# Second half of the output in one bank for each token block, the last in quarters; final sums of two blocks on ScalarE and GpSimd; eight gate stores from GpSimd's queue

## The chip, the core and the metric

The kernel runs on one core of a Trainium2 chip. A core has TensorE (matrix products, PE in the profile, with its weight loads as PEld), VectorE (DVE), ScalarE (ACT), GpSimd (POOL) and SyncE (SP), which here only issues DMAs. TensorE writes its products to PSUM, eight banks of 128 partitions by 512 float32; the other tiles lie in SBUF. Each engine works through its own instructions in order; semaphores join them. The metric is the time of one execution on the device in microseconds.

## What is computed

One layer of a hybrid encoder over 2048 tokens of width 1024, with 16 learned tokens ahead. The reference, cut:

```python
u = rms_norm(h, pre_g)
proj = u @ w_in
glu_a, glu_b, conv_gate, q, k, v, sb_gate = jnp.split(proj, ..., axis=-1)
c = glu_a * jax.nn.sigmoid(glu_b)
c = causal_depthwise_conv(c, conv_w, conv_b)                 # width 31
c = jax.nn.silu(layer_norm(c, conv_ln_g, conv_ln_b))
c = (c @ w_pw2 + b_pw2) * jax.nn.silu(conv_gate)
s = stick_breaking_attention(heads(q), heads(k), heads(v))   # 8 heads of 64
s = s.reshape(...) * jax.nn.silu(sb_gate)
mixed = jnp.concatenate([c, s], axis=-1) @ w_out
return h + rms_norm(mixed, post_g)
```

The change touches the last two lines for the last 512 tokens, and the storing of `silu(sb_gate)`.

## The kernel before

The tokens are worked in four chunks of 512 (`TC`). For each chunk there are input projections, convolution, attention over all keys so far, and the output projection. A float32 product is made of three passes: both factors are split in a high and a low part (ScalarE rounds, VectorE or GpSimd subtracts; "hi", "lo"), and high x high, high x low and low x high are added in one PSUM bank. In the profile every instruction has line 218, that of a recording helper; operations are told apart by their tiles.

The order of the instructions comes from a planner that runs when the program is built. It keeps an estimated time for each engine and merges two streams of TensorE work, the attention and a filler (projections, convolution, output projection); small jobs on other engines are put in with `when` once their inputs are expected. The order is thus fixed in the program.

*PSUM.* The eight banks are four tags (`BANKS`): "mm" 2, "T" 4, "av" 1, "cv" 1. "av" holds a head's attention sum, "cv" the running convolution while there is one.

*Gates.* `sb_gate(c)` (line 1073) projects the four gates of chunk c; each is stored to `gscr` in DRAM (line 1079) by SP's queue, which also loads weights ("wr", "w"), keys and values. They are read back much later.

*The end of the last chunk.* The mixed input has eight blocks of 128 channels; the last one (k = 7, heads 6 and 7) comes last, so everything else is done ahead of it. `out_part` (line 1600) sums the first seven blocks: for output columns 0 to 511 into SBUF ("tok"), for columns 512 to 1023 in `late` (line 1621) into PSUM banks that stay open. There a bank holds 256 columns (`OC`) of two token blocks of 128 tokens: `late(0)` fills "cv" and "mm" for blocks 0 and 1, `late(1)` "mm" and "T" for blocks 2 and 3. The second is run in part before and in part inside `out_last`.

`out_last` (line 1631) runs when the last mixed block is there, in the order written at lines 1691 to 1714: `first(tb)` multiplies the last block for columns 0 to 511, `second(i)` adds it to the open banks of blocks 2i and 2i + 1. `add_first` adds the bank to "tok", ScalarE squares it with a sum over the row ("sq"), VectorE multiplies by the gain ("uh", `post_g`); `add_second` squares and multiplies two pieces of 256 from the banks. `rate` adds the four partial sums (VectorE) and takes the power -0.5 (GpSimd, "st"). `give_out` makes the final sum `y * rate + x` on VectorE, two halves of 512 columns in "ul", and stores each by SP.

Two instructions on different engines that read one bank are kept apart by semaphores: VectorE's multiplication waits for ScalarE's square of the same bank.

Of the kernel before, what the change touches and what calls it, by code (L numbers as in the profile page):

```python
# [14 lines left out]
AF = mybir.ActivationFunctionType  # L15
ALU = mybir.AluOpType
# [3 lines left out]
P = 128  # L20
D = 1024
KD = D // P
SEQ = 2048
NM = 16
TC = 512
NCH = SEQ // TC
NTB = TC // P
# [7 lines left out]
OC = 256  # L35
# [231 lines left out]
def trunk(ctx: ExitStack, tc: tile.TileContext, x, xturn, xlater, meta, cpack, post_g, wpack, out):  # L267
# [16 lines left out]
    def when(what, ins, outs=(), engine=None, date=0.0, tag=None):  # L284
        soon.append(Later(clock, what, ins, outs, engine, date, tag))

    pe = Engine(clock, nc.tensor, pe_cost, 0.15, run)
    dve = Engine(clock, nc.vector, dve_cost, 0.04, run)
    act = Engine(clock, nc.scalar, act_cost, 0.04, run)
    pool = Engine(clock, nc.gpsimd, pool_cost, 0.04, run)  # L290
    sp = Engine(clock, nc.sync, sp_cost, 0.0, run)
# [24 lines left out]
    def T(tag, shape, bufs, dt=F32):  # L316
        room(tag, bufs)
        t = sb.tile(shape, dt, tag=tag, name=tag, bufs=bufs)
        clock.take(tag, bufs, t.name)
        return t  # L320

    def PT(tag, shape):
        bufs = BANKS[tag]
        room(tag, bufs)
        t = ps.tile(shape, F32, tag=tag, name=tag, bufs=bufs)
        clock.take(tag, bufs, t.name)
        return t
# [3 lines left out]
    def need(*aps, tag=None, given=None, evs=0, n=1):  # L331

        def at():
            if given and not given():
                return 1e6
            t = max([clock.at(a) for a in aps] + [0.0])
            if tag:
                t = max(t, clock.next_free(tag, n))  # L340
            if evs:

                t = max(t, clock.next_free("ev", evs) - 1.0)
            return t + slack[0]

        return at
# [6 lines left out]
    o = NJ * CW  # L353
# [116 lines left out]
    def finish_off(pieces):  # L470

        while True:
            try:
                next(pieces)
            except StopIteration as e:
                return e.value
# [116 lines left out]
    def release():  # L593
        held.pop()
        tags.popleft()
        prepare()
# [476 lines left out]
    def sb_gate(c):  # L1073
        for j in range(NJ):
            def ev_g(pt, o, n):
                sg = ev()[:, :TC]
                act.activation(sg, pt, AF.Sigmoid)
                dve.tensor_tensor(sg, pt, sg, op=ALU.mult)
                when(lambda j=j: sp.dma_start(gscr[c, j], sg), [sg], ["g"])

            yield from proj(c, G_SG + j, ev_g, False)

# [2 lines left out]
    keep = {("z", -1): True}  # L1085
# [487 lines left out]
    def out_products(w, mix, ks, half, whole=True, bank=None, there=None, tag="mm", free=None):  # L1573


        fresh = bank is None
        for i, k in enumerate(ks):
            wh, wl = (t[:, k % 2, :] for t in w[k // 2])
            if k % 2 == 0:
                pair = ks[i : i + 2]  # L1580
                if there:
                    yield need(given=lambda: all(there(kk) for kk in pair))
                nxt = [m for kk in pair for m in mix(kk)]
                yield need(wh, wl, *nxt, tag=None if bank is not None else tag)
            if bank is None:
                bank = PT(tag, [P, 2, OC])
            for b in range(2):
                tb = 2 * half + b
                mh, ml = (t[:, tb * P : (tb + 1) * P] for t in mix(k))
                o = bank[:, b, :]  # L1590


                pe.matmul(o, mh, wh, start=(fresh and i == 0 and b == 0), stop=False)
                pe.matmul(o, mh, wl, start=False, stop=False)
                pe.matmul(o, ml, wh, start=False, stop=(whole and i == len(ks) - 1 and b == 1))
            if (half if free is None else free) and (k % 2 or i == len(ks) - 1):
                release()
        return bank

    def out_part(y, c):  # L1600

        yield need(given=lambda: ("conv", c) in keep)
        mix = lambda k: mixc[c][k] if k < NJ else mixs[c][k - NJ]
        there = lambda k: k < NJ or k - NJ in mixs[c]
        for n in range(0, D // 2, OC):
            w = weights(w_out, n, OC, 0, KD - 1)
            ks, banks = range(KD - 1), [None, None]
            if n == 0:  # L1610

                for i in range(2):
                    banks[i] = yield from out_products(
                        w, mix, range(KD - 2), i, False, there=there
                    )
                ks = range(KD - 2, KD - 1)
            for i in range(2):
                b = yield from out_products(w, mix, ks, i, True, banks[i], there)
                act.activation(y[i][:, :, n : n + OC], b, AF.Copy)

        def late(i, tags):
            for e in range(2):
                w = weights(w_out, D // 2 + e * OC, OC, 0, KD - 1)
                keep["o", i, e] = yield from out_products(
                    w, mix, range(KD - 1), i, False, tag=tags[e], free=True
                )

        yield from late(0, ("cv", "mm"))
        keep["rest"] = late(1, ("mm", "T"))

    def out_last(y, mh, ml):


        def products(o, tb, wh, wl, start, stop):
            h, l = (t[:, tb * P : (tb + 1) * P] for t in (mh, ml))
            pe.matmul(o, h, wh, start=start, stop=False)
            pe.matmul(o, h, wl, start=False, stop=False)
            pe.matmul(o, l, wh, start=False, stop=stop)

        pg = keep["pg"]  # L1640
        w0, w1 = keep["w", 0], keep["w", 1]
        sums, rates = T("sq2", [P, NTB, 4], 1), {}
        pool.memset(sums[:, :, 3:], 1e-6)

        def first(tb):
            a = PT("T", [P, TC])
            products(a, tb, *w0, True, True)
            return a

        def second(i):  # L1650
            for e in range(2):
                for b in range(2):
                    w = (t[:, e * OC : (e + 1) * OC] for t in w1)
                    products(keep["o", i, e][:, b], 2 * i + b, *w, False, b == 1)

        def square(tb, src, n):
            junk = T("ev", [P, TC], EV, BF16)[:, : src.shape[1]]

            act.activation(
                junk, src, AF.Square, scale=D ** -0.5, accum_out=sums[:, tb, n : n + 1]  # L1660
            )

        def add_first(tb, a):

            yt = y[tb // 2][:, tb % 2, 0:TC]
            dve.tensor_tensor(yt, yt, a, op=ALU.add)
            square(tb, yt, 0)
            dve.tensor_tensor(yt, yt, pg[:, 0], op=ALU.mult)

        def add_second(tb):  # L1670
            yt = y[tb // 2][:, tb % 2, TC:]
            for e in range(2):
                o, cols = keep["o", tb // 2, e][:, tb % 2], slice(e * OC, (e + 1) * OC)
                square(tb, o, 1 + e)
                dve.tensor_tensor(yt[:, cols], o, pg[:, 1, cols], op=ALU.mult)

        def rate(tb):
            ss, rates[tb] = T("ss", [P, 1], 2), T("st2", [P, 1], 8)
            dve.tensor_reduce(ss, sums[:, tb], axis=mybir.AxisListType.X, op=ALU.add)
            pool.tensor_tensor(rates[tb], ss, nhalf, op=ALU.pow)  # L1680

        def give_out(tb):
            for h in range(2):
                xr, cols = keep["x"][:, 2 * tb + h], slice(h * TC, (h + 1) * TC)
                dve.scalar_tensor_tensor(
                    xr, y[tb // 2][:, tb % 2, cols], rates[tb], xr, op0=ALU.mult, op1=ALU.add
                )
                t0 = (NCH - 1) * TC + tb * P
                sp.dma_start(out[t0 : t0 + P, cols], xr)

        rest = keep["rest"]
        for _ in range(3):
            next(rest)
        a = [first(0)]
        second(0)
        a += [first(tb) for tb in range(1, NTB)]
        add_first(0, a[0])
        finish_off(rest)
        second(1)
        add_second(0)  # L1700
        add_first(1, a[1])
        rate(0)
        add_second(1)
        add_first(2, a[2])
        rate(1)
        give_out(0)
        add_first(3, a[3])
        give_out(1)
        add_second(2)
        rate(2)  # L1710
        add_second(3)
        rate(3)
        give_out(2)
        give_out(3)

    def out_proj(c, mixc, mixs):
# [262 lines left out]
```

## Time and profile before

| | |
|---|---|
| median of 3 runs | 1321.98 us (1319.52 to 1323.74) |
| profiled execution | 1323.13 us |
| its span | 1321.4 us |
| TensorE busy, mean granted clock | 1294.5 us, 0.996 |
| VectorE, ScalarE, GpSimd busy | 1013.1, 735.3, 659.0 us |

The span is what the trace covers of the execution. A row of the timeline gives start and length in us, engine, line, operation, tiles written and read, shape, count, and in brackets the engine's idle time before it with what ended it. A row of the groups gives count, total and mean time of one in ns, and the idle time before. TensorE is busy in nearly the whole span and idle in the last 14.4 us, in which the other engines normalize and store the last blocks.

### The profile page before, as it was taken

The page shows a single profiled execution, that of the slowest core. Times are in us where ns is not written, and L with a number is a line of the kernel's source. Part 1 is how long each engine was busy: PE and PEld are TensorE (multiplying, and loading weights), DVE is VectorE, ACT ScalarE, POOL GpSimd, SP SyncE. Part 2 cuts the span into 40 slices and gives each one's busy share as a digit, 9 for nine tenths or more (in the row PEclk, how much of TensorE's full clock was granted, in tenths as well). Part 3 has the DMA queues.
Part 4 walks back from the last instruction along what each step waited for, and adds up shares of the span by engine and source line. Part 5 has one row for each costly group of instructions (what it writes and reads, how often), then busy time and mean ns, then how long its engine had stood idle before and what let it go on. Part 6 is the DMA issues. An engine that isn't in the chain of part 4 may idle for free.

```text
span 1321.4 us, 21882 instructions
## 1 busy us (share of the span) xinstructions
PE 1294.5 (98%) x7498; PEld 1114.0 (84%) x7498; DVE 1013.1 (77%) x1439; ACT 735.3 (56%) x1469; POOL 659.0 (50%) x779
## 2 busy tenths in 40 slices
PE   8999999999999999999999999999999999999995
PEld 8998878888799888888889988888778898988895
DVE  4999988989973498974585578985549998798854
ACT  6544464444455452667644544677776666655532
POOL 2555468777667430778821332588786121232300
PEclk9999999999999999999999999999999999999998
DMA  6687878899868996677756696667666446686644
GB/s 229 216 260 231 249 244 271 291 334 333 289 223 274 311 304 196 204 233 214 243 162 195 206 323 209 186 189 217 209 196 213 143 152 177 199 277 207 199 153 144
DMA packets 167471, 300.77 MB, mean 228 GB/s; under 512 B 17840, under 2 KB 72304, under 8 KB 167360
## 3 DMA queue, kind: packets, MB, share of 16 engines
q1 hardware_dynamic: 154208, 253.49, 62.1%
q0 software_dynamic: 13152, 45.88, 9.1%
q8 instruction: 59, 0.97, 0.3%
q14 instruction: 52, 0.43, 0.1%
HBM read 221.85 MB, written 77.46 MB: 227 GB/s over the span
## 4 chain that ended last, share of the span: by engine, by line
PE 86%; DVE 5%; DMA 4%; ACT 1%; POOL 1%; issue 1%; SPq 0%; DVEq 0%; ACTq 0%; POOLq 0%
PE mm L218 56%; PE T L218 21%; PE av L218 9%; DVE ul L218 2%; DMA ev<-x 2%; DVE tok L218 1%; DVE pr L218 1%; POOL acc L218 1%; DMA tok<-xlater 1%; DMA w<-wscr 0%; ACT ev L218 0%; DMA out<-tok 0%; DVE cv L218 0%; PE cv L218 0%; DMA tok<-gscr 0%
## 5 line engine op out<-in xcount | busy, mean ns | idle before, releaser
L218 PE MATMUL mm<-uh,w 128*128 128x512 f32 (+1 forms) x1936 | 619.2, 377 | 1.8 <-ACT uh L218 1.8
L218 PEld LDWEIGHTS mm<-uh,w 128*128 128x128 f32 x1936 | 353.1, 190 | 61.8 <-ACT uh L218 2.2
L218 PE MATMUL mm<-ul,w 128*128 128x512 f32 (+1 forms) x968 | 361.0, 373 | 1.1 <-DVE ul L218 1.0
L218 DVE TENSOR_TENSOR al<-T,ah 128x512 fp32r<-128x512 f32 (+3 forms) x323 | 194.5, 602 | 132.8 <-ACT ah L218 131.4
L218 DVE TENSOR_TENSOR_SCAN pr<-T,pr,zcol 128x512 f32<-128x512 f32 x192 | 245.4, 1278 | 50.9 <-ACT T L218 48.5
L218 ACT ACTIVATE ah<-T 128x512 fp32r<-128x512 f32 (+3 forms) x323 | 171.6, 532 | 182.6 <-PE T L218 180.8
L218 DVE SCALAR_TENSOR_TENSOR cv<-ct,cp,cv 128x512 f32<-128x512 f32 x319 | 239.2, 750 | 6.9
L218 POOL TENSOR_TENSOR w<-wr,w 128x512 fp32r<-128x512 f32 x132 | 171.3, 1302 | 92.7 <-ACT w L218 90.1
L218 POOL TENSOR_TENSOR acc<-acc,pd 128x512 f32<-128x512 f32 x150 | 195.5, 1303 | 43.4 <-ACT pd L218 31.5
L218 ACT ACTIVATE T<-T 128x512 f32<-128x512 f32 (+2 forms) x320 | 167.3, 524 | 86.6 <-PE T L218 77.8
L218 PEld LDWEIGHTS mm<-ul,w 128*128 128x128 f32 x968 | 183.6, 190 | 27.5 <-DVE ul L218 2.1
L218 PE MATMUL T<-kk,q 128*128 128x512 f32 (+2 forms) x640 | 195.2, 388 | 1.6 <-DVE pr L218 1.6
L218 PE MATMUL T<-ident,pr 128*128 128x128 f32 x1088 | 171.2, 272 | 0.7 <-DVE tok L218 0.6
L218 PEld LDWEIGHTS T<-ident,pr 128*128 128x128 f32 x1088 | 134.3, 140 | 32.1 <-DVE tok L218 1.0
L218 DVE TENSOR_TENSOR_SCAN pr<-T,tri 128x128 f32<-128x128 f32 (+3 forms) x128 | 103.9, 815 | 22.4 <-ACT T L218 21.8
L218 PEld LDWEIGHTS T<-kk,q 128*128 128x128 f32 x640 | 105.2, 189 | 15.6 <-DVE pr L218 2.5
L218 PE MATMUL av<-ah,vk 128*128 128x512 f32 (+1 forms) x320 | 116.7, 365 | 0.3 <-ACT ev L218 0.2
L218 PE MATMUL av<-al,vk 128*128 128x512 f32 (+1 forms) x320 | 116.9, 366 | 0.0
L218 ACT ACTIVATE pd<-ct,cp 128x512 f32<-128x512 f32 x150 | 106.4, 717 | 15.6 <-POOL acc L218 14.8
L218 ACT ACTIVATE w<-wr 128x512 fp32r<-128x512 f32 x140 | 86.3, 626 | 34.3 <-PE mm L218 13.0
L218 POOL COPY cm<-pr 128x1 f32<-128x1 f32 x120 | 24.4, 204 | 142.3 <-DVE pr L218 141.6
L218 POOL TENSOR_TENSOR ev<-ev 64x512 f32<-64x512 f32 (+2 forms) x46 | 55.9, 1216 | 75.9 <-ACT ev L218 43.8
(194 smaller groups left out, 1572.3 us busy)
## 6 DMA issues: line engine op xcount, KB each, us to landing
w<-wscr SPq DMA_DIRECT2D x150, 512.0 KB, 4.1
wr<-wpack SPq DMA_DIRECT2D x140, 256.0 KB, 4.6
wscr<-w POOLq DMA_DIRECT2D x68, 512.0 KB, 4.8
kk<-kscr SPq DMA_DIRECT2D x80, 256.0 KB, 4.7
vk<-vscr SPq DMA_DIRECT2D x80, 256.0 KB, 4.1
q<-qscr SPq DMA_DIRECT2D x64, 256.0 KB, 5.6
vscr<-mixs SPq DMA_DIRECT2D x32, 256.0 KB, 3.1
qscr<-ehl SPq DMA_DIRECT2D x32, 256.0 KB, 2.8
```

Of the source, the lines that this page charges most:

```text
L218: return call(out, *args, **kw)
```

## The change

It has three parts.

1. `late` gives each token block a bank of its own with all 512 columns: blocks 0 and 1 in "cv" and "mm", block 2 in "mm", block 3 in quarters of the output row: columns 512 to 767 in "av", 768 to 1023 in "cv". The last part of the products runs first for block 2, which is finished with block 3's first quarter, then for block 3's last quarter alone.
2. In `out_last`, `add_first` writes its sum back to the bank and squares it there; `add_second` works on 512 columns (block 3: 256); the final sums of blocks 0 and 1 are a scaling on ScalarE and an addition on GpSimd.
3. The gate stores of chunks 2 and 3 are issued by GpSimd.

```diff
@@ sb_gate
-                when(lambda j=j: sp.dma_start(gscr[c, j], sg), [sg], ["g"])
+                q = pool if c > 1 else sp
+                when(lambda j=j: q.dma_start(gscr[c, j], sg), [sg], ["g"])
@@ late
             for e in range(2):
                 w = weights(w_out, D // 2 + e * OC, OC, 0, KD - 1)
-                keep["o", i, e] = yield from out_products(
-                    w, mix, range(KD - 1), i, False, tag=tags[e], free=True
-                )
+                for bs in ([0], [1]) if i and e else ([0, 1],):
+                    for k in range(KD - 1):
...
+                        for b in bs:
+                            tb = 2 * i + b
+                            fresh = k == 0 and (e == 0 or tb == NTB - 1)
+                            if fresh:
+                                tag = tags[b + e]
+                                yield need(tag=tag)
+                                bank = PT(tag, [P, TC])
+                                for n in range(e, 2):
+                                    keep["o", tb, n] = bank
+                            mh, ml = (t[:, tb * P : (tb + 1) * P] for t in mix(k))
+                            o = keep["o", tb, e][:, e * OC : (e + 1) * OC]
+                            pe.matmul(o, mh, wh, start=fresh, stop=False)
+                            pe.matmul(o, mh, wl, start=False, stop=False)
+                            pe.matmul(o, ml, wh, start=False, stop=False)
...
+                    if bs == [0]:
+                        keep["second"](2 * i)
+                        keep["second"](2 * i + 1, 0)
+                        keep["ended"] = 2 * i
-        yield from late(0, ("cv", "mm"))
-        keep["rest"] = late(1, ("mm", "T"))
+        yield from late(0, ("cv", "mm"))
+        keep["rest"] = late(1, ("mm", "av", "cv"))
@@ out_last
         def add_first(tb, a):
             yt = y[tb // 2][:, tb % 2, 0:TC]
-            dve.tensor_tensor(yt, yt, a, op=ALU.add)
-            square(tb, yt, 0)
-            dve.tensor_tensor(yt, yt, pg[:, 0], op=ALU.mult)
+            dve.tensor_tensor(a, yt, a, op=ALU.add)
+            square(tb, a, 0)
+            dve.tensor_tensor(yt, a, pg[:, 0], op=ALU.mult)
...
-        def give_out(tb):
+        def give_out(tb, apart=False):
...
+                if apart:
+                    act.activation(yt, yt, AF.Copy, scale=rates[tb])
+                    pool.tensor_tensor(xr, xr, yt, op=ALU.add)
+                else:
+                    dve.scalar_tensor_tensor(xr, yt, rates[tb], xr, op0=ALU.mult, op1=ALU.add)
...
+        keep["second"] = second
+        for _ in range(5):
             next(rest)
         a = [first(0)]
         second(0)
+        second(1)
         a += [first(tb) for tb in range(1, NTB)]
         add_first(0, a[0])
-        finish_off(rest)
-        second(1)
+        while "ended" not in keep:
+            next(rest)
         add_second(0)
+        rate(0)
         add_first(1, a[1])
-        rate(0)
         add_second(1)
+        rate(1)
+        give_out(0, True)
         add_first(2, a[2])
-        rate(1)
-        give_out(0)
         add_first(3, a[3])
-        give_out(1)
+        give_out(1, True)
         add_second(2)
         rate(2)
-        add_second(3)
+        add_second(3, 0)
+        finish_off(rest)
+        second(3, 1)
+        give_out(2)
+        add_second(3, 1)
         rate(3)
-        give_out(2)
         give_out(3)
```

How the instructions then stand. VectorE's last ones before the change, from the last sum of a first half ("tok<-tok,T") on; "st" is a block's rate, "sq" the sums of squares, "uh" the gain, "ul" the result, and "waits" names the engines waited for:

```order
L218 TENSOR_TENSOR tok<-tok,T 128x512 [waits PE_49]
L218 TENSOR_TENSOR tok<-tok,uh 128x512 [waits Activation_49]
...
L218 TENSOR_TENSOR tok<-mm,uh 128x256 [waits Activation_49]
L218 TENSOR_TENSOR tok<-T,uh 128x256 [waits Activation_49]
L218 TENSOR_REDUCE ss<-sq_15234 128x1
L218 SCALAR_TENSOR_TENSOR ul<-tok,st_15417,ul 128x512 [waits Pool_49]
L218 SCALAR_TENSOR_TENSOR ul<-tok,st_15417,ul 128x512 [waits DVE_49]
L218 SCALAR_TENSOR_TENSOR ul<-tok,st_15427,ul 128x512 [waits Pool_49]
L218 SCALAR_TENSOR_TENSOR ul<-tok,st_15427,ul 128x512 [waits DVE_49]
```

And after it, from the last sum of a first half:

```order
L218 TENSOR_TENSOR T<-tok,T 128x512 [waits PE_49]
L218 TENSOR_TENSOR tok<-T,uh 128x512 [waits Activation_49]
L218 TENSOR_TENSOR tok<-mm,uh 128x512 [waits Activation_49]
L218 TENSOR_REDUCE ss<-sq_15234 128x1 [waits Pool_49]
L218 TENSOR_TENSOR tok<-av,uh 128x256 [waits Activation_49]
L218 SCALAR_TENSOR_TENSOR ul<-tok,st_15380,ul 128x512 [waits Pool_49]
L218 SCALAR_TENSOR_TENSOR ul<-tok,st_15380,ul 128x512 [waits DVE_49]
L218 TENSOR_TENSOR tok<-cv,uh 128x256 [waits Activation_49]
L218 TENSOR_REDUCE ss<-sq_15234 128x1
L218 SCALAR_TENSOR_TENSOR ul<-tok,st_15419,ul 128x512 [waits Pool_49]
L218 SCALAR_TENSOR_TENSOR ul<-tok,st_15419,ul 128x512 [waits DVE_49]
```

Two final sums (block 2's) now stand ahead of the gain and the sum of block 3's last quarter, and four in all are gone from VectorE.

GpSimd's last instructions after the change (before it there were only the four "st"):

```order
L218 MEMSET sq_15234 128x4 [waits Pool_49]
L218 TENSOR_TENSOR st_15342<-ss,nhalf 128x1 [waits DVE_49]
L218 TENSOR_TENSOR st_15353<-ss,nhalf 128x1 [waits DVE_49]
L218 TENSOR_TENSOR ul<-ul,tok 128x512 [waits Activation_49] x4
L218 TENSOR_TENSOR st_15380<-ss,nhalf 128x1 [waits DVE_49]
L218 TENSOR_TENSOR st_15419<-ss,nhalf 128x1 [waits DVE_49]
```

The four additions of blocks 0 and 1 stand between the second and the third power.

ScalarE's last instructions after the change, from block 0's first square on ("ev" takes the squares, which nobody reads):

```order
L218 ACTIVATE ev,sq_15234<-T 128x512 [waits DMAHW7_49,DMASW5_49,DVE_49]
L218 ACTIVATE ev,sq_15234<-cv 128x512 [waits PE_49]
L218 ACTIVATE ev,sq_15234<-T 128x512 [waits DVE_49]
L218 ACTIVATE ev,sq_15234<-mm 128x512 [waits DMAHW4_49,DMASW1_49,PE_49]
L218 ACTIVATE tok<-tok,st_15342 128x512 [waits Pool_49]
L218 ACTIVATE tok<-tok,st_15342 128x512
L218 ACTIVATE ev,sq_15234<-T 128x512 [waits DMAHW5_49,DMAHW3_49,DVE_49]
L218 ACTIVATE ev,sq_15234<-T 128x512 [waits DVE_49,Activation_49]
L218 ACTIVATE tok<-tok,st_15353 128x512 [waits Pool_49]
L218 ACTIVATE tok<-tok,st_15353 128x512
L218 ACTIVATE ev,sq_15234<-mm 128x512 [waits PE_49,Activation_49]
L218 ACTIVATE ev,sq_15234<-av 128x256 [waits PE_49,Activation_49]
```

Before, ScalarE had only squares here; the scalings of a block ("tok<-tok,st") now stand among them, block 1's behind the first-half squares of blocks 2 and 3.

More of the change, by code (lines that the diff above doesn't have):

```diff
@@ L1623, in late @@
                 w = weights(w_out, D // 2 + e * OC, OC, 0, KD - 1)
-                keep["o", i, e] = yield from out_products(
-                    w, mix, range(KD - 1), i, False, tag=tags[e], free=True
-                )
+                for bs in ([0], [1]) if i and e else ([0, 1],):
+                    for k in range(KD - 1):
+                        wh, wl = (t[:, k % 2, :] for t in w[k // 2])
+                        if k % 2 == 0:
+                            pair = range(k, min(k + 2, KD - 1))
+                            yield need(wh, wl, *(m for kk in pair for m in mix(kk)))
+                        for b in bs:
[12 more added lines that the diff above has]
+                            pe.matmul(o, ml, wh, start=False, stop=False)
+                        if bs[-1] and (k % 2 or k == KD - 2):
+                            release()
+                    if bs == [0]:
+                        keep["second"](2 * i)
+                        keep["second"](2 * i + 1, 0)
+                        keep["ended"] = 2 * i
         yield from late(0, ("cv", "mm"))
-        keep["rest"] = late(1, ("mm", "T"))
+        keep["rest"] = late(1, ("mm", "av", "cv"))
     def out_last(y, mh, ml):
@@ L1642, in out_last @@
         sums, rates = T("sq2", [P, NTB, 4], 1), {}
+        pool.memset(sums[:, :, 2:], 0.0)
         pool.memset(sums[:, :, 3:], 1e-6)
@@ L1648, in first, with second @@
             return a
[L1650 to L1654, printed above, removed]
+        def second(tb, e=None):
+            cols = slice(0, TC) if e is None else slice(e * OC, (e + 1) * OC)
+            o = keep["o", tb, e or 0][:, cols]
+            products(o, tb, *(t[:, cols] for t in w1), False, True)
         def square(tb, src, n):
@@ L1665, in add_first, with add_second @@
             yt = y[tb // 2][:, tb % 2, 0:TC]
-            dve.tensor_tensor(yt, yt, a, op=ALU.add)
-            square(tb, yt, 0)
-            dve.tensor_tensor(yt, yt, pg[:, 0], op=ALU.mult)
[L1670 to L1675, printed above, removed]
+            dve.tensor_tensor(a, yt, a, op=ALU.add)
+            square(tb, a, 0)
+            dve.tensor_tensor(yt, a, pg[:, 0], op=ALU.mult)
+        def add_second(tb, e=None):
+            cols = slice(0, TC) if e is None else slice(e * OC, (e + 1) * OC)
+            o = keep["o", tb, e or 0][:, cols]
+            square(tb, o, 1 + (e or 0))
+            dve.tensor_tensor(y[tb // 2][:, tb % 2, TC:][:, cols], o, pg[:, 1, cols], op=ALU.mult)
         def rate(tb):
@@ L1680, in rate @@
             pool.tensor_tensor(rates[tb], ss, nhalf, op=ALU.pow)
-        def give_out(tb):
+        def give_out(tb, apart=False):
             for h in range(2):
                 xr, cols = keep["x"][:, 2 * tb + h], slice(h * TC, (h + 1) * TC)
-                dve.scalar_tensor_tensor(
-                    xr, y[tb // 2][:, tb % 2, cols], rates[tb], xr, op0=ALU.mult, op1=ALU.add
-                )
+                yt = y[tb // 2][:, tb % 2, cols]
+                if apart:
[3 more added lines that the diff above has]
+                    dve.scalar_tensor_tensor(xr, yt, rates[tb], xr, op0=ALU.mult, op1=ALU.add)
                 t0 = (NCH - 1) * TC + tb * P
@@ L1691, in out_last @@
         rest = keep["rest"]
-        for _ in range(3):
+        keep["second"] = second
+        for _ in range(5):
             next(rest)
```

## The prediction

> **What bounds the kernel now.** I read the page first, then the busy time by stretches, then who made TensorE wait, and last the timeline of the end.
>
> ```profile
> span 1321.4 us, 21882 instructions
> PE 1294.5 (98%) x7498; PEld 1114.0 (84%) x7498; DVE 1013.1 (77%) x1439; ACT 735.3 (56%) x1469; POOL 659.0 (50%) x779
> 640.00:700.00 60.00, 60.00 (x360) 52.04 (x359) 48.98 (x72) 32.19 (x67) 26.84 (x33) 1.00 0.66 208
> 985.00:1045.00 60.00, 59.45 (x329) 49.71 (x328) 53.99 (x71) 40.33 (x78) 30.17 (x32) 1.00 0.62 197
> 1290.00:1321.40 31.40, 16.99 (x134) 16.28 (x132) 15.29 (x33) 6.92 (x26) 3.09 (x4) 0.84 0.40 140
> ```
>
> TensorE is busy for 98% of the span. The three rows give length, then TensorE, its weight loads, VectorE, ScalarE and GpSimd. The first two stretches are those in which the moved gate stores of chunks 2 and 3 stand: TensorE is idle for 0.00 and 0.55 us there. The third is the end: TensorE idles 14.4 of 31.4 us. So the change can gain only at the end, unless it makes TensorE wait elsewhere.
>
> ```profile
> 1306.11 0.88 PE L218 MATMUL T<-acc,mixs 128*128 128x256 f32 x6
> 1308.30 0.15 DVE L218 TENSOR_REDUCE ss<-sq 128x1 f32<-128x4 f32 x1
> 1308.53 0.55 POOL L218 TENSOR_TENSOR st<-ss,nhalf 128x1 f32<-128x1 f32 x1 [4.53 <-DVE ss L218]
> 1309.37 2.73 DVE L218 SCALAR_TENSOR_TENSOR ul<-tok,st,ul 128x512 f32<-128x512 f32 x4
> ```
>
> This is the timeline of the end (start, length, engine, operation). The last product ends at 1306.99. Then VectorE works off its own queue: the last two blocks' gains, two sums, and four final sums that end at 1312.10. From there to 1321.40 are 9.3 us of last store, its landing and the program's end; nothing of that changes, since the last store still follows the last final sum. **Only the 5.1 us from 1306.99 to 1312.10 can shrink.**
>
> **The change part by part.** *Products.* The same columns are multiplied.
>
> ```profile
> 1289.89 0.63 DVE L218 SCALAR_TENSOR_TENSOR uh<-av,vcol,uh 64x128 f32<-64x128 f32 x2
> 1291.39 2.96 PE L218 MATMUL mm<-w,mixc 128*128 128x256 f32 x24
> 1294.19 0.86 PE L218 MATMUL T<-acc,mixs 128*128 128x512 f32 x3
> 1295.08 0.69 DVE L218 TENSOR_TENSOR tok<-tok,T 128x512 f32<-128x512 f32 x1 [2.81 <-PE T L218]
> 1295.80 0.63 ACT L218 ACTIVATE ev<-tok 128x512 bf16<-128x512 f32 x1 [3.98 <-DVE tok L218]
> 1296.34 0.19 ACT L218 ACTIVATION_READ_ACCUMULATOR ev<-tok 128x1 f32 x1
> 1296.43 0.36 ACT L218 ACTIVATE ev<-cv 128x256 bf16<-128x256 f32 x1
> 1296.56 0.69 DVE L218 TENSOR_TENSOR tok<-tok,uh 128x512 f32<-128x512 f32 x1 [0.79 <-ACT ev L218]
> 1297.17 0.42 DVE L218 TENSOR_TENSOR tok<-cv,uh 128x256 f32<-128x256 f32 x1
> 1297.50 0.42 DVE L218 TENSOR_TENSOR tok<-mm,uh 128x256 f32<-128x256 f32 x1
> 1298.39 2.26 PE L218 MATMUL mm<-w,mixs 128*128 128x256 f32 x18
> 1300.49 2.96 PE L218 MATMUL T<-wr,mixc 128*128 128x256 f32 x24
> ```
>
> 18 products of 256 columns take 1300.49 - 1298.39 = 2.10 us, 0.117 each; three of 512 take 0.69 (1294.19 to 1294.88). Nine of 512 replace eighteen of 256 in the second halves: 2.07 for 2.10. I take the end of the products at 1306.9. What moves is when each block is complete. From 1298.39, 39 products of 256 and three of 512 (4.56 + 0.69) give block 2's second half at about 1303.7; three of 256 more give the first quarter of block 3 at 1304.1; only 21 + 3 products (2.8 us) for the last quarter stand behind. The new bank "av" is read until 1290.52 (1289.89 + 0.63); its first product follows the first three of those that now start at 1291.39, at 1291.74, so I expect no wait of TensorE.
>
> *First two blocks.* The final sums of blocks 0 and 1 (four on VectorE) become four ScalarE scalings and four GpSimd additions. The rows nearest to them, and to the sums that are now written to a bank:
>
> ```profile
> L218 DVE TENSOR_TENSOR T<-T,tok 128x512 f32<-128x512 f32 x12 | 8.2, 686 | 0.2 <-PE T L218 0.2
> 992.77 0.71 ACT L218 ACTIVATE pd<-ct,cp 128x512 f32<-128x512 f32 x1
> 993.38 0.59 ACT L218 ACTIVATE T<-T 128x512 f32<-128x512 f32 x1
> 1006.25 2.55 POOL L218 TENSOR_TENSOR mixs<-tok,mixs 128x512 fp32r<-128x512 f32 x2
> L218 POOL TENSOR_TENSOR tok<-tok,vcol 128x512 f32<-128x512 f32 x12 | 12.3, 1038 | 0.9 <-DMA tok<-sscr 0.9
> L218 POOL TENSOR_TENSOR mixc<-mixc 128x512 fp32r<-128x512 f32 x12 | 17.1, 1428 | 20.0 <-ACT mixc L218 20.0
> 1302.85 1.41 DVE L218 SCALAR_TENSOR_TENSOR ul<-tok,st,ul 128x512 f32<-128x512 f32 x2
> 1303.01 0.99 POOL L218 TENSOR_TENSOR st<-ss,nhalf 128x1 f32<-128x1 f32 x1 [2.30 <-DVE ss L218]
> ```
>
> A sum into a bank costs VectorE 0.69 as into "tok". A square of 512 columns with its accumulator takes 0.73 to its reader and 0.63 to the next instruction (rows above); one read from a bank isn't there at 512 columns: I keep 0.63, and 0.59 (the last of the pair at 992.77, a 512 from a bank) is the low end. A scaling by a column takes 0.71, the next starts after 0.61. Two additions on GpSimd: 2.55 (two of one row), between 2.08 (1038 each) and 2.86 (1428 each). The rate's power is 0.55 or 0.99 on GpSimd.
>
> Now the queues, from 1295.05, with 0.03 from engine to engine and 0.08 from a sum to GpSimd (1308.45 to 1308.53). VectorE still waits for each square before it multiplies by the gain, since both read one bank.
> - Block 0: sum 1295.08, squares 1295.80 and 1296.43, gains to 1297.88, rate on GpSimd 1298.02 to 1298.57.
> - Block 1: sum to 1298.55, squares 1298.58 and 1299.21, gains to 1300.66, rate 1300.80 to 1301.35.
> - Block 0's scalings stand behind block 1's squares on ScalarE: 1299.84 to 1301.17. Its additions: 1301.40 to 1303.95.
> - First halves of blocks 2 and 3: sum 1300.64, square 1301.36 to 1302.09, gain to 1302.81, sum 1302.72, square 1303.44 to 1304.17.
> - Block 1's scalings can only follow: 1304.07 to 1305.40. **So its additions start at 1304.86, and two of them end at 1307.41.**
> - Block 2's second half is squared at 1305.29, multiplied to 1306.74, summed by 1306.80. Its power, though, stands behind the four additions in GpSimd's queue: 1307.43 to 1307.98.
> - VectorE's two final sums of block 2: 1308.01 to 1309.42 (1.41). Only behind them come the gain of block 3's last quarter (0.33 to the next instruction, as from 1297.17 to 1297.50), its sum and the power: 1309.88 to 1310.43. Two final sums more: to 1311.88.
>
> The last final sum ends at 1311.9 instead of 1312.1: **0.2 us earlier.** What VectorE is relieved of (four final sums, 2.8 us) comes back as a wait for GpSimd, and the early last quarter lies ready at 1307.4 without being taken up.
>
> Bounds of this sum: additions at 1038 each save another 0.5, six squares at 0.59 save 0.24 (in all 0.9 earlier than before); additions at 1428 cost 0.3 and two powers at 0.99 cost 0.88 (in all 1.0 later). I take 0.55 for the powers because beside the power of 0.99 VectorE ran final sums (1302.85), beside that of 0.55 none, and in the new order nothing of that kind stands beside a power. The Trainium skill, "SBUF — State Buffer", section "SBUF: two separate sides", has the rule: a VectorE instruction with two SBUF inputs and a GpSimd one that reads SBUF hold a shared pair of ports exclusively, and the later one waits. By that rule the powers stay at 0.55 and the sum is -0.2; if 0.99 were the power's own cost it would be +0.7. The rows agree with the rule.
>
> *Gate stores.* Eight stores of chunks 2 and 3 go from SP's queue to GpSimd's.
>
> ```profile
> SPq L218 <- DVE ev L218: 2.6, 3, 1.1
> PE T L218 <- POOL ev L218: 1.1, 2, 0.6
> PE mm L218 <- DMA w<-wscr: 0.7, 1, 0.7
> PE T L218 <- DVE tok L218: 0.6, 1, 0.6
> PE T L218 <- DVE pr L218: 0.2, 1, 0.2
> L218 POOL DMA_DIRECT2D sscr<-ev x30 | 16.9, 562 | 8.9 <-POOL ev L218 8.6 <-DMA ev<-post_g 0.3
> 645.93 1.28 POOL L218 TENSOR_TENSOR w<-wr,w 128x512 fp32r<-128x512 f32 x1 [0.49 <-ACT w L218]
> 659.66 0.48 PE L218 MATMUL mm<-uh,w 128*128 128x512 f32 x1
> 1008.75 6.84 POOL L218 TENSOR_TENSOR acc<-acc,pd 128x512 f32<-128x512 f32 x5
> 1035.76 0.60 PE L218 MATMUL T<-ident,acc 128*128 128x128 f32 x4
> ```
>
> The first row is SP's waiting for gates from 600 to 1060 us (2.6 us in three waits), the next four all of TensorE's waits from 640 to 1060. For a load TensorE waited once, 0.7 us, so a freed SP is worth between 0 and 0.7; I take 0. GpSimd pays 562 ns per issue (the row of its other stores), 4.5 us in all, at times with a wait for the gate, as SP has now (1.1 at most). Behind it queue weight splits and taps of the convolution. The split of 645.93 is read by TensorE at 659.66, 12.4 us after its end; the last tap ends at 1015.59, 20.2 us before it is transposed. Single delays of about 1 us vanish in that. I take 0, and 4.5 as the upper end.
>
> The sum: -0.2 us on the profiled execution, whose time is 1323.13 with a span of 1321.4. The median of the runs shown is 1321.98, 1.15 below it, so I set 1321.98 - 0.2 = **1321.8 us**.
>
> **The rivals.**
> - *The end is set by TensorE alone* (GpSimd's queue is not in the way, the change does all it can): after 1306.9 a square of 256 and its accumulator (0.46), a gain (0.42), sum, power and two final sums (0.08 + 0.08 + 0.55 + 1.41) end at 1310.0: 2.1 us earlier, 1319.9. For it: everything else of block 3 is ready by then. Against it: the additions of block 1 wait for scalings that stand behind the square of block 3. 14%.
> - *Slower: GpSimd holds still at the gate stores* and TensorE runs out of split weights. It decides once a hold outlasts the 12.4 us lead; if then every issue goes through to TensorE, it costs eight times 0.56, 4.5 us: 1326.3. Against it: the stores GpSimd issues already take 562 ns each. The Trainium skill, "SBUF — State Buffer", section "SBUF: two separate sides", warns that GpSimd writes the descriptors of its own DMAs and can be locked out of that by VectorE; the row of 562 ns shows nothing of this, so the rule adds nothing to the chance. 7%.
> - *The change doesn't do what it says at the end*: powers and additions are held up by neighbours, at the upper bounds above, and the end comes 1.0 us later: 1323.0. 9%.
>
> **How the numbers follow.** Forecast (end within about half a microsecond of before, stores free) 70%; the rivals 14, 7 and 9%. A difference under 0.3%, 4.0 us, can hardly be told from no change. No case but the second reaches it by itself: all that can shrink is 5.1 us, and TensorE's chain alone leaves 3.0 of it. The runs of before spread from 1319.52 to 1323.74, which counts for a median too. Range 1319.0 to 1325.0: it takes in the first and third rival and a scatter of some 2 us, and leaves out the second. Faster 5%, same 88%, slower 7%.
>
> **What would show it.** In the changed profile: the last product near 1306.9; the four additions of GpSimd back to back or waiting for ScalarE, ending near 1307.4; the third power right after them; VectorE idle between the gain of block 3's first quarter (near 1307) and its final sums (1308); the last final sum near 1311.9, 9.3 before the span's end. The stretches 640 to 700 and 985 to 1045 keep TensorE idle for under 1 us. I am wrong if the third power comes right behind its sum, if TensorE shows new waits for GpSimd's splits or for the bank "av", or if the last product shifts by a microsecond or more.

## The result, and the profile after

| | before | after |
|---|---|---|
| median | 1322.15 us (1319.41 to 1323.74, 7 runs) | 1317.51 us (1316.01 to 1318.72, 7 runs) |
| ratio | | 0.9962 (0.9952 to 0.9973) |
| profiled execution, span | 1323.13, 1321.4 us | 1318.22, 1316.5 us |

The change makes the kernel 0.38% faster, some 4.6 us. The forecast was 1321.8 us, with a range whose lower end was 1319.0. One execution of a later kernel (the eight copies) took 1589.29 us at a granted clock of 0.753, and its ratio leaves that execution out. The page and the busy time by stretches of the changed kernel (length, then TensorE, its weight loads, VectorE, ScalarE, GpSimd):

```profile
span 1316.5 us, 21862 instructions
PE 1295.0 (98%) x7489; PEld 1113.7 (85%) x7489; DVE 1012.0 (77%) x1432; ACT 736.8 (56%) x1467; POOL 667.6 (51%) x792
...
640.00:700.00 60.00, 60.00 (x360) 52.04 (x359) 48.97 (x72) 32.19 (x67) 29.07 (x37) 1.00 0.65 207
985.00:1045.00 60.00, 59.15 (x327) 49.47 (x326) 53.77 (x71) 40.03 (x78) 32.21 (x36) 1.00 0.63 196
1290.00:1316.50 26.50, 17.16 (x127) 16.06 (x125) 12.83 (x27) 8.61 (x24) 7.23 (x8) 0.90 0.50 172
```

TensorE is as busy as before (1295.0 against 1294.5 us), and in the stretches with the moved stores it idles 0.00 and 0.85 us. The whole gain of the span, 4.9 us, is in the last stretch: TensorE idles 9.3 us there, against 14.4. The timeline of the changed kernel's end:

```profile
1294.45 0.86 PE L218 MATMUL T<-acc,mixs 128*128 128x512 f32 x3
...
1304.98 2.55 POOL L218 TENSOR_TENSOR ul<-ul,tok 128x512 f32<-128x512 f32 x2 [0.98 <-ACT tok L218]
...
1306.65 0.51 PE L218 MATMUL cv<-acc,mixs 128*128 128x256 f32 x3
...
1307.49 0.55 POOL L218 TENSOR_TENSOR st<-ss,nhalf 128x1 f32<-128x1 f32 x1
...
1308.07 1.42 DVE L218 SCALAR_TENSOR_TENSOR ul<-tok,st,ul 128x512 f32<-128x512 f32 x2 [0.86 <-POOL st L218]
...
1309.96 0.55 POOL L218 TENSOR_TENSOR st<-ss,nhalf 128x1 f32<-128x1 f32 x1 [1.93 <-DVE ss L218]
1310.55 1.41 DVE L218 SCALAR_TENSOR_TENSOR ul<-tok,st,ul 128x512 f32<-128x512 f32 x2 [0.66 <-POOL st L218]
```

The last final sum ends at 1311.96, against 1312.10 before. So the engines' work ends 0.14 us earlier, and the span ends 4.9 us earlier: the gain lies *behind* the last computing instruction, where 9.3 us have become 4.5. What SyncE waited for there, first before, then after (line 1975 or 2007 is the program's end, and "q" behind an engine's name means its instruction queue; us in total, times, longest):

```profile
SPq L1975 <- PEq L1975: 6.5, 2, 6.0
SPq L1975 <- DMA out<-ul: 1.6, 1, 1.6
```

```profile
SPq L2007 <- DMA out<-ul: 2.7, 1, 2.7
SPq L2007 <- PEq L2007: 0.6, 2, 0.5
```

Before, the landing of the last store cost SyncE 1.6 us, and then it waited 6.0 us at a barrier, where the engines wait for one another. The view names TensorE's sequencer, but TensorE's last product had ended at 1306.99. The instructions of the end itself (duration in ns least, median, longest; first and last start) name the late one. Before, then after:

```profile
L1975 POOLq DRAIN  x3: 40/102/11079, 1309.5 to 1321.1; - x3
L1975 SPq DRAIN  x3: 7/7/7, 1314.7 to 1320.8; - x3
```

```profile
L2007 POOLq DRAIN  x3: 40/93/1576, 1309.9 to 1316.2; - x3
L2007 SPq DRAIN  x3: 7/7/7, 1315.6 to 1315.9; - x3
```

Each engine has instructions called DRAIN in its closing part. The first of GpSimd's three starts at 1309.5 and takes 11.08 us before the change, to 1320.6; SyncE had reached its own at 1314.7. After the change it takes 1.58 us, to 1311.5, and the end comes as soon as SyncE has its landings (1315.6). **The gain is this DRAIN.** It doesn't wait for a transfer to land: GpSimd's last one before the change was issued at 1215.17 and landed 3.7 us later. In the two profiled executions the landing cost SyncE 1.1 us more after the change (2.7 against 1.6), so that some 4.9 of the 6.0 us are left as gain. What shortened the DRAIN, the profile doesn't tell: the change alters GpSimd's last work, its neighbours on VectorE, and the number of stores that it issues.

### The profile page after: what moved, and what is told of

Same layout as the page of the kernel before. It is cut to its first block, busy times and chain, and to the rows that moved or that the text cites. A ratio compares the mean times of both kernels' runs of the same rounds, so it can differ in the third digit from the quotient of the medians.

```text
span 1316.5 us, 21862 instructions
## 1 busy us (share of the span) xinstructions
PE 1295.0 (98%) x7489; PEld 1113.7 (85%) x7489; DVE 1012.0 (77%) x1432; ACT 736.8 (56%) x1467; POOL 667.6 (51%) x792
## 4 chain that ended last, share of the span: by engine, by line
PE 85%; DVE 7%; DMA 3%; issue 2%; POOL 2%; ACT 2%; SPq 0%; DVEq 0%; POOLq 0%; ACTq 0%
PE mm L218 54%; PE T L218 21%; PE av L218 9%; DVE cv L218 3%; DVE ul L218 1%; DMA wr<-wpack 1%; DVE tok L218 1%; POOL acc L218 1%; ACT ev L218 1%; DMA w<-wscr 0%; DVE pr L218 0%; POOL ev L218 0%; DMA sscr<-ev 0%; PE cv L218 0%; DMA pr<-xturn 0%
```

## The experiments

**First group: which part of the change shortens the DRAIN.** Three theories: neighbours (N; my first guess, since GpSimd's last power and the DRAIN stood beside VectorE's final sums), GpSimd's additions shortly before (A), the moved stores (S).

The change without its moved stores:

```diff
-                q = pool if c > 1 else sp
+                q = sp
```

> The changed kernel with its eight gate stores back in SP's queue. After the last final sum the span still had 9.3 us before the change and 4.5 us behind it, and GpSimd's closing DRAIN took 11.08 us before and 1.58 behind it. Theory N (neighbours): the DRAIN is long where GpSimd's last power and the DRAIN stand beside VectorE's final sums as they did before; the stores have no part in it, so the DRAIN stays near 1.6 us and the time near 1317.5 us (ratio about 0.996). Theory S (stores): the eight stores from GpSimd's queue shorten the DRAIN; it is 11 us again here and the time near 1322 us (ratio about 1.000). Theory A (additions): what GpSimd did in the last 50 us, the final sums' additions, keeps the DRAIN short; here 1317.5 us as in N.

Only the moved stores:

```diff
-                when(lambda j=j: sp.dma_start(gscr[c, j], sg), [sg], ["g"])
+                q = pool if c > 1 else sp
+                when(lambda j=j: q.dma_start(gscr[c, j], sg), [sg], ["g"])
```

> The kernel before with only the gate stores moved to GpSimd's queue. Theories N and A: DRAIN about 11 us, time about 1322 us (1.000). Theory S: DRAIN about 1.6 us, time about 1317.5 us (0.996).

Only the final sums of the first two blocks:

```diff
-                dve.scalar_tensor_tensor(
-                    xr, y[tb // 2][:, tb % 2, cols], rates[tb], xr, op0=ALU.mult, op1=ALU.add
-                )
+                yt = y[tb // 2][:, tb % 2, cols]
+                if tb < 2:
+                    act.activation(yt, yt, AF.Copy, scale=rates[tb])
+                    pool.tensor_tensor(xr, xr, yt, op=ALU.add)
+                else:
+                    dve.scalar_tensor_tensor(xr, yt, rates[tb], xr, op0=ALU.mult, op1=ALU.add)
```

> The kernel before with only this part of the change: the final sums of blocks 0 and 1 on ScalarE (times rate) and GpSimd (plus x); banks and order as before. The last power still stands beside VectorE's final sums of block 2 (rate of block 3 comes ahead of them). Theory N: DRAIN about 11 us, time 1321 to 1323 us. Theory A: DRAIN about 1.6 us, time 1317 to 1318.5 us. Theory S: as N.

The kernel before, with GpSimd's last work put behind VectorE's last final sum:

```diff
                 sp.dma_start(out[t0 : t0 + P, cols], xr)
+            if tb == NTB - 1:
+                pool.tensor_tensor(T("ss", [P, 1], 2), xr[:, 0:1], nhalf, op=ALU.add)
```

> The kernel before with one more GpSimd instruction at the very end: an addition on 128x1 that reads the last final sum, its result unused. GpSimd's DRAIN can then finish only after VectorE's last final sum (about 1312.1) and that addition (about 0.55). Theory N: nothing stands beside GpSimd's last work, the DRAIN ends near 1314, SP's landings (about 1315) decide, time about 1317 us (0.996). Theories A and S: the DRAIN stays about 10 us behind GpSimd's last work, ends near 1323, time 1323.5 to 1325 us (1.001 to 1.002).

Measured: the change without the stores 1322.31 us, ratio 0.9998 (0.9989 to 1.0008); the stores alone 1317.82, 0.9966 (0.9951 to 0.9980); the final sums alone 1321.83, 0.9996 (0.9986 to 1.0005); the held GpSimd 1324.44, 1.0016 (1.0007 to 1.0025). The program's end of the change without stores, and of the stores alone:

```profile
L2007 POOLq DRAIN  x3: 40/93/10641, 1309.0 to 1320.2; - x3
L2007 SPq DRAIN  x3: 7/7/7, 1313.6 to 1319.9; - x3
```

```profile
L1976 POOLq DRAIN  x3: 40/102/2012, 1309.9 to 1315.7; - x3
L1976 SPq DRAIN  x3: 7/7/7, 1315.1 to 1315.4; - x3
```

Theory S holds in all four, and the stores alone account for the whole result. N falls: in the kernel with the stores alone the last power runs beside VectorE's final sums as it did before (0.99 us), and the DRAIN is short; in the held kernel nothing stands beside GpSimd's last work, and the DRAIN is long. A falls: with the additions and without the stores it is long.

The held kernel shows something more. The DRAIN's own length is no good measure, since it starts while GpSimd's last instruction still runs or waits. Counted from the end of that instruction, it ran on for 10.05 us before (the last power 1309.53 to 1310.52, the DRAIN to 1320.57), and for 10.05 in the three kernels of this group with a long one, whenever the last instruction came. So it looks like a fixed amount of work and not like a wait for another engine.

**Second group: what about the stores matters.** GpSimd's transfers in the trace of before:

```profile
wscr<-w POOLq DMA_DIRECT2D x68, 512.0 KB, 4.8
...
out<-tok POOLq DMA_DIRECT2D x24, 256.0 KB, 5.7
...
sscr<-ev POOLq DMA_DIRECT2D x30, 128.0 KB, 4.0
```

These are 122; the change adds eight. The four kernels differ from before in the line of the gate store, `q = pool if c > 2 else sp` (four stores moved), `q = pool if c < 2 else sp` (the eight early ones), all on `pool`, and, for the fourth, a second copy beside the stores of SyncE:

```diff
                 when(lambda j=j: sp.dma_start(gscr[c, j], sg), [sg], ["g"])
+                if c > 1:
+                    when(lambda j=j: pool.dma_start(gtwo[c, j], sg), [sg], ["h"])
```

> The kernel before with only the four gate stores of the last chunk on GpSimd's queue (126 transfers issued by GpSimd in the trace, against 122 before and 130 with eight). What is open is how eight stores shorten GpSimd's closing DRAIN from 11 to about 2 us. Theory C (count): the number of transfers that GpSimd has issued decides, as a threshold or a remainder; the DRAIN is then either 11 us (time 1322) or about 2 us (1318), or something between if it goes by the number. Theory L (late work): GpSimd's transfers in the last chunks decide; with four in the last chunk the DRAIN is short, 1318 us. Theory R (relief): what counts is that SP's queue has fewer transfers; with four fewer the DRAIN is between 2 and 11 us.

> The kernel before with the eight gate stores of the first two chunks on GpSimd's queue, those of the last two on SP's (130 transfers of GpSimd). Theories C and R: DRAIN about 2 us, time about 1318 us. Theory L: DRAIN 11 us, time about 1322 us. Costs of the early stores themselves on GpSimd and SP, at most 1 us, would stand in TensorE's idle time, not in the DRAIN.

> The kernel before with all sixteen gate stores on GpSimd's queue (138 transfers). Theory C as a threshold, theories L and R: DRAIN about 2 us, time about 1318 us. Theory C as a remainder: a DRAIN of another length, up to 11 us and 1322 us.

> The kernel before with its sixteen gate stores on SP, and a second copy of the last two chunks' eight gates stored by GpSimd's queue to a place in DRAM that nothing reads (130 transfers of GpSimd, none fewer of SP). Theories C and L: DRAIN about 2 us, time about 1318 us. Theory R: DRAIN 11 us, time about 1322 us.

Measured: four 0.9998 (0.9986 to 1.0010); the eight early 0.9945 (0.9926 to 0.9965); sixteen 0.9963 (0.9947 to 0.9978); eight copies 0.9952 (0.9928 to 0.9976). The rows of four and of sixteen:

```profile
L1976 POOLq DRAIN  x3: 40/102/11406, 1308.2 to 1320.1; - x3
```

```profile
L1975 POOLq DRAIN  x3: 40/102/2829, 1309.6 to 1315.4; - x3
```

L and R fall. The early stores do as well as the late ones, copies that relieve SyncE of nothing do as well as moved stores, and four late stores make the DRAIN longer by 0.3 us. What is left of the three is C: the DRAIN goes with the transfers that GpSimd has issued, with a jump between 126 and 130, and a small growth on either side of it.

**Third group: the growth, the jump, and its unit.** The 24 output stores of the earlier chunks on SyncE (98 transfers left on GpSimd):

```diff
-                lambda: pool.dma_start(out[t0 : t0 + P, i * 512 : i * 512 + 512], o), [o]
+                lambda: sp.dma_start(out[t0 : t0 + P, i * 512 : i * 512 + 512], o), [o]
```

> The kernel before with the 24 output stores of the earlier chunks on SP's queue instead of GpSimd's (98 transfers issued by GpSimd). So far GpSimd's DRAIN ran past its last other instruction by 10.05 us with 122 transfers, 10.4 with 126, 1.0 with 130 and 1.8 with 138. Theory P (proportional): the DRAIN clears the transfers issued since an earlier clearing, about 0.08 us each (10.05 over 122); here 98 x 0.082 = 8.1 us past the last power, so the DRAIN ends near 1318.6 and the time is about 2 us shorter than before, near 1320.3 (0.9985), unless SP's queue makes TensorE wait. Theory F (fixed): below some number the DRAIN takes 10 us whatever the number; time 1322 us (1.000).

Six gate stores moved, `q = pool if c > 2 or (c == 2 and j > 1) else sp`:

> The kernel before with six gate stores on GpSimd's queue, the last chunk's four and two of the third (128 transfers of GpSimd). Theory P with a clearing in the course of the program once some number is reached: if that number is 127 or 128, the DRAIN runs about 0.8 us past the last power, time about 1318 us; if it is 129 or 130, about 10.5 us, time about 1322.5 us. Theory F allows either length but none between.

Eight tiny transfers added:

```diff
                 when(lambda j=j: sp.dma_start(gscr[c, j], sg), [sg], ["g"])
+                if c > 1:
+                    when(lambda j=j: pool.dma_start(gtwo[c, j], sg[0:16, 0:16]), [sg], ["h"])
```

> The kernel before with its sixteen gate stores on SP, and eight more transfers of GpSimd of 16x16 values (1 KB) each out of the last two chunks' gates to a place in DRAM that nothing reads: 130 transfers of GpSimd, but with few more packets (130 transfers of a gate's size brought 13792 packets, against 13152 before). If GpSimd's clearing goes by the number of transfers: DRAIN about 1 us past the last power, time about 1317 us. If it goes by packets or bytes: about 10 us past it, time about 1322 us.

The change with the other eight stores, `q = pool if c < 2 else sp`:

> The changed kernel with the eight gate stores of the first two chunks on GpSimd's queue in place of those of the last two. The number of GpSimd's transfers is the same 130, so the DRAIN stays near 1.6 us and the end waits for SP's landings. If the place of the stores costs nothing: 1317.5 us (0.996). The kernel before with the stores of the first two chunks was at 0.9945 (0.9926 to 0.9965); if that was more than chance, 1315 to 1316 us here.

Measured: 98 transfers 1320.16 us, 0.9985 (0.9976 to 0.9995), as forecast by theory P (8.1 us past the last power, 1320.3); six 1316.48, 0.9959 (0.9944 to 0.9973); eight tiny ones 1315.55, 0.9952 (0.9934 to 0.9970, two executions); the change with early stores 1315.9, 0.9953 (0.9940 to 0.9965). The rows of 98 transfers and of the eight tiny ones:

```profile
L1975 POOLq DRAIN  x3: 40/102/9117, 1309.3 to 1318.9; - x3
```

```profile
L1978 POOLq DRAIN  x3: 40/102/1851, 1309.2 to 1315.0; - x3
```

All kernels by their transfers ("past" is from the end of GpSimd's last other instruction to the end of its DRAIN, worked out from the starts and durations in the trace; "from the stop on" is explained below):

| GpSimd's transfers | from the stop on | kernel | past, us | ratio |
|---|---|---|---|---|
| 98 | no stop | fewer | 8.10 | 0.9985 |
| 122 | no stop | before | 10.05 | 1 |
| 122 | no stop | change without stores; sums alone; held | 10.05 each | 0.9998, 0.9996, 1.0016 |
| 126 | no stop | four | 10.38 | 0.9998 |
| 128 | 2 | six | 0.83 | 0.9959 |
| 130, eight tiny | 2 | tiny | 0.83 | 0.9952 |
| 130 | 4 | change; stores alone; early; copies | 0.99 each | 0.9962, 0.9966, 0.9945, 0.9952 |
| 130 | 4 | change with early stores | 0.99 | 0.9953 |
| 138 | 14 | sixteen | 1.81 | 0.9963 |

From 98 to 122 a transfer adds 0.081 us (1.95 over 24), from 122 to 126 0.08; 98 and 122 times 0.082 give nearly the whole length. So the DRAIN seems to work off something left by each transfer, and with 128 or more most of it is gone by then. The jump doesn't go by the bytes: eight transfers of 1 KB bring it as eight of 256 KB do. Nor does it go by the packets of GpSimd's queue: there are 13408 with the eight tiny transfers, fewer than the 13472 with four stores, where the DRAIN stayed long.

Where it went, and when, can be read in part. GpSimd's timeline near 1180 us, without the moved stores (the first fence) and of the change:

```profile
1179.01 0.54 POOL L218 DMA_DIRECT2D sscr<-ev  x1 [0.29 <-POOL ev L218]
1179.54 0.57 POOL L218 DMA_DIRECT2D out<-tok  x1
1180.42 0.54 POOL L218 DMA_DIRECT2D out<-tok  x1 [0.31 <-DVE al L218]
```

```profile
1179.90 0.54 POOL L218 DMA_DIRECT2D sscr<-ev  x1 [0.29 <-POOL ev L218]
1183.23 1.12 POOL L218 DMA_DIRECT2D out<-tok  x2 [2.79 <-DVE al L218]
```

The first `out<-tok` here is GpSimd's 119th transfer without the stores and its 127th in the change. Without them it follows at once; in the change it starts 2.79 us late, though the transfers there stand in the same order. The view names VectorE's "al", for which the same transfer didn't wait without the stores; its data ("tok") were complete at 1178.21, the end of VectorE's sum that starts at 1177.49. With six stores the 127th is another transfer (it starts at 1187.34, behind 6.14 us of idle time, where without the stores it stood behind 3.26), and with the eight tiny ones it is the 129th. With all sixteen stores it is the 125th, near 1041 us. That transfer with the stores alone (the first fence), and with sixteen:

```profile
1038.84 0.55 POOL L218 DMA_DIRECT2D sscr<-ev  x1 [0.30 <-POOL ev L218]
```

```profile
1041.32 0.57 POOL L218 DMA_DIRECT2D sscr<-ev  x1 [3.13 <-issue]
```

Here the view finds nothing that GpSimd waited for ("issue"), and the transfer is 2.83 us late. So GpSimd stops once, in each of the eight kernels with 128 transfers or more, and in none of the six with 126 or fewer. The length of the DRAIN then goes by the transfers from the delayed one on, as in the table: from 4 to 14 it grows by 0.82 us, again 0.08 for each, with some 0.66 us on top (an estimate from these rows). That the DRAIN is longer with sixteen stores than with eight fits this: the stop comes sooner there. What makes GpSimd stop is not the number of transfers alone, nor the packets alone: it stopped after 126 transfers and 13504 packets of its queue with six stores, after 124 and 13504 with sixteen, and after 128 and 13280 with the eight tiny ones. A stop of under 3 us takes some 9.5 us off the DRAIN (10.38 to 0.83), so it isn't the same work done sooner at the same pace; what is done in it isn't seen. The stop costs nothing here: in the change GpSimd's next work for others comes at the usual time (a copy at 1188.44, against 1188.22 before).

None of these kernels is shown to beat the change. The lowest ratio, 0.9945 with the early stores, has an interval that overlaps the change's, and so has the 0.9953 of the change with early stores (1315.9 us, inside the 1315 to 1316 that was expected if the early place is worth something). Whether it is worth something stays open; the kernels were timed in different comparisons.

## Why the prediction was wrong

- *TensorE bounds the kernel, and only the end can gain*: right. TensorE is busy 98% as before, its idle time in both stretches is under 1 us (0.00 and 0.85), and the gain is in the last stretch.
- *Products and the new bank "av"*: right. TensorE's last part starts 0.26 us later than before (1294.45 against 1294.19); the last product ends at 1307.16, forecast 1306.9 from the earlier start. No wait for "av" stands in it.
- *The queues of the end*: right step by step (the forecast in brackets). Block 1's additions start at 1304.98 (1304.86) and end at 1307.53 (1307.41); the third power comes right behind them at 1307.49 (1307.43); VectorE idles 0.86 us for it; the last final sum ends at 1311.96 (1311.88). Powers with no final sum beside them took 0.55, as taken. Forecast 0.2 us earlier than before, measured 0.14. That the new banks and final sums are worth nothing that can be measured is borne out by the change without the stores, 0.9998.
- *"From there to 1321.40 are 9.3 us of last store, its landing and the program's end; nothing of that changes, since the last store still follows the last final sum"*: **this step failed.** Of the 9.3 us only 2.6 were store and landing (1312.10 to 1314.7). Then SyncE, and with it the end, waited for GpSimd's DRAIN, to 1320.57, which has nothing to do with the last store: it ran past GpSimd's own last instruction by 10.05 us. In the change that is 0.99, and the 9.3 us are 4.5. The DRAIN was the last wait of the program before, and with it short the landing is.
- *The bound "only the 5.1 us from 1306.99 to 1312.10 can shrink"* fell with it: the last final sum came only 0.14 us earlier, and 4.8 us went behind it, where nothing was to shrink.
- *Gate stores at 0, between a gain of 0.7 and a loss of 4.5*: right for the middle of the program, which is all I looked at, and wrong in the sum. Their price was at the end, a gain of some 4.6 us (0.9966 with the stores alone), through the transfers that GpSimd issues. Without the DRAIN in the sum the fastest rival ended at 1319.9 us, and none could reach 1317.51.

The waits of SyncE at the end and the row of the DRAIN were there to be read in the trace of before: a 6.0 us wait that was not for a landing. That eight more stores would take it away could not be read there. But one could read there that 6 us of the end belonged to something other than the store, and that should have been a rival and a wider range.

## What to carry to other kernels

The stretch behind the last computing instruction is a chain like any other: ask which engine's closing instruction ends last, and don't put it down to the last store's landing. Where an engine issues DMAs, moving them can have a price at the program's end too: here GpSimd's closing DRAIN grew by some 0.08 us for each transfer it had issued, up to 126 of them, and was over 8 us shorter than before with 128 to 138. When a change has several parts, run each alone first: here the large one (new banks, new order, other engines) gave nothing, and one line on a queue gave all.

## What the runs showed of the hardware that was not expected

- GpSimd's closing DRAIN took 8.1 us past its last instruction with 98 transfers issued, 10.05 with 122, 10.38 with 126, and 0.8 to 1.8 with 128 to 138. In the kernels with 128 or more, and only there, GpSimd once started a transfer 2.8 to 2.9 us late, and the DRAIN then went by the transfers from that one on (0.83 us with 2, 0.99 with 4, 1.81 with 14). That each transfer leaves work, and that the stop clears what the ones before it left, is the reading which fits the runs; the clearing itself is not in the trace. Open is what triggers the stop: it came at the 127th transfer with 128 or 130, at the 129th when eight are tiny, at the 125th with 138.
- GpSimd's DRAIN starts before its last instruction has run, so its printed length holds a wait as well: 2.01 us with the stores alone and 1.58 in the change, with the same 1.0 us past the last power.
